# Two attention mixers with heads interleaved, one aligned slab pool and one more held chunk of output weights

## The chip, the cores and the metric

The kernel runs on one NeuronCore of one Trainium2 chip, as one program. The time is device time of that core, in microseconds, the median of several executions. The engines are TensorE (PE, matrix products), its weight loader (PEld in the profile), VectorE (DVE), ScalarE (ACT), GpSimd (POOL) and SyncE (SP), which issues most of the DMA transfers here. Each engine takes its own instructions strictly in the order in which they stand in its queue.

## The reference

The program computes two transformer blocks of two layers each on 512 tokens of width 1024, all in fp32. The second block has besides a context of 256 tokens. What the change touches lies in the second block, whose first layer mixes tokens with a window attention (8 heads, beside a Fourier mix), and whose second layer mixes them with a neighbourhood attention (16 heads). Cut to that:

```python
def _window_attention(q, k, v, k_ctx, v_ctx, sink):      # first layer ("even")
    ...
    s_win = jnp.einsum('bnqkgd,bnjkd->bnkgqj', qb, kw).astype(jnp.float32) * scale
    s_ctx = jnp.einsum('bnqkgd,bjkd->bnkgqj', qb, k_ctx).astype(jnp.float32) * scale
    ...
    p = jax.nn.softmax(jnp.concatenate([s_win, s_ctx, sk], axis=-1), axis=-1).astype(v.dtype)
    o = (jnp.einsum('bnkgqj,bnjkd->bnqkgd', p[..., :nw], vw)
         + jnp.einsum('bnkgqj,bjkd->bnqkgd', p[..., nw:nw + C], v_ctx))

def _neighbourhood_attention(q, k, v, k_ctx, v_ctx, rel_bias):   # second layer ("odd"), per row r of 64 tokens
    ...
        s_nb = jnp.einsum('bqhd,bjhd->bhqj', q_row, k_rows).astype(jnp.float32) * scale + bias[None]
        s_nb = jnp.where(mask[None, None], s_nb, NEG_2)
        s_cx = jnp.einsum('bqhd,bjhd->bhqj', q_row, k_ctx).astype(jnp.float32) * scale
        p = jax.nn.softmax(jnp.concatenate([s_nb, s_cx], axis=-1), axis=-1).astype(v.dtype)
        return (jnp.einsum('bhqj,bjhd->bqhd', p[..., :n], v_rows)
                + jnp.einsum('bhqj,bjhd->bqhd', p[..., n:], v_ctx))

    for i in range(DEPTH):                                # second_block
        ...
        x = x + g1 * o
        h = _rms(x, norm2_g[i]) * (1.0 + sc2) + sh2
        x = x + g2 * _swiglu(h, ffn_w_gate[i], ffn_w_up[i], ffn_w_down[i])
```

The context heads (`_ctx_attention`) attend from the 256 context tokens to themselves, in the first layer alone. `o` is the attention's output times an output matrix of 1024 x 1024 (`ev_w_out`, `od_w_out`).

## The kernel before

**Products.** An fp32 product is made of three products of rounded halves: every operand is split into a high half (a cast on ACT) and the rest (a subtraction on DVE), and `mm3` (L188 to L192) multiplies high by high (L190), high by low (L191) and low by high (L192). Weights come from HBM in pieces of 128 x 1024 into four raw buffers `wr`; `weight` (L145) issues the load on SP, casts to `wh` on ACT (L160) and subtracts to `wl` on DVE (L161), three buffers each. With `held=True` the halves go to slabs instead and stay. `split` (L169, its two instructions L172 and L173) does the same for activations: `xq` are split inputs of a projection, `mgh`, `hdh`, `yah`, `ybh`, `ycl` split intermediate results of the first block (h and l for the halves), `cath` and `catl` split outputs of attention, `pth` and `ptl` split transposed softmax weights.

**PSUM.** Eight banks of 128 x 512: four with tag A for attention, four with tag G for projections.

**Stages in time.** First block: mixer to 560 us, FFN to 950, mixer to 1510, FFN to 1925. Second block: the even layer's context heads until 2030 or so, its window attention 2070 to 2245, the rest of its mixer to 2375, its FFN to 2720, a transition to 2775; the odd mixer's attention in four groups of four heads that begin at 2771, 2854, 2937 and 3020, the end of its mixer 3110 to 3145, its FFN 3145 to 3500.

**Filling.** Attention leaves PE gaps while softmax runs on the other engines. So the projections for the next group are written as generators in a queue; `fill(us)` (L128) draws matmuls from it until so many microseconds, by the code's own rates, are used up. Where `fill` stands in the code decides what stands between two steps of attention on PE; the scheduler that builds the program then may move single instructions.

**An odd head** (`s1` L1472, `s2` L1514, the loop behind it). `s1` makes scores for four query tiles: two stacked products of 256 columns each (L433, L434) into one bank, neighbourhood keys in its left half and context keys in its right; DVE adds mask and bias and takes the maximum in one instruction; ACT makes the exponentials (one of 512 columns, L1498, for tiles 0 and 3; two of 256, L1504 and L1506, for tiles 1 and 2); then `fill(0.85)`. The bias of a head is loaded by three DMAs and prepared on GpSimd (L1481). The operands are *stacks*: every two heads, `stacks` transposes queries and keys (ten blocks) and splits them on ACT and DVE into 128-row tiles `stk` and `low` (L403 and after). `s2` calls `window_av` (L1012) for the head before: two context blocks and three window blocks, each of them transposes of exponentials into one bank (L1020 or L1029), split into `pth` and `ptl`, `fill(0.85)`, and the products with the values into one bank `po` that is held for the whole head (L1024 or L1038). `fold` then copies `po` into `ya` (L482), and after each second head `over_sums` divides by the sums. In the loop all four score blocks of a head come first and then the five blocks of the head before; groups do not overlap: the last head of a group has its `window_av` alone.

**The output matrix of the odd layer.** Its 1024 rows are four chunks `w[hf, 0..3]` for each half `hf` of the columns. Chunks 0 to 2 need the heads of groups 0 to 2 and are multiplied as filling in the last group (`out_part`); chunk 3 is loaded and split there, and multiplied in `out_end`, two half-chunks for each of four token tiles and two halves, after the last head. Behind each tile come its residual sum, its norm and its transposes (L298) for the FFN.

**The even layer's heads** (`heads` L1288 with `c1`, `c2` for the context and `s1`, `s2` for the window) run the same way, with fills of 2.0 and 3.0 us, and 1.3 us. In the window attention each of the four query tiles has two banks of scores, two maxima and two exponentials.

**Slabs.** `phase` opens one pool a stage; `F` gives slabs of 128 x 512 fp32, `R` the same for split halves, each tag with its own number of buffers (`MIX1`, `FFN1` and so on). Small tiles are in the same pool. In the program as built `wh`, `wl` and `xq` begin at 64 bytes past a multiple of 128 in each partition; the slabs of the first block begin at a multiple of 128, those of the even mixer and of the second block's FFNs at 64 past it.

Of the kernel before, what the change touches and what calls it, by code (L numbers as in the profile page):

```python
# [9 lines left out]
F32 = mybir.dt.float32  # L10
# [31 lines left out]
FFN1 = dict(F=18, R=34)  # L42
FFN1B = dict(F=17, R=28)
CF = (2.0, 3.0)
EVEN = dict(F=21, R=25, L=2)
FFN2 = dict(F=18, R=30)
ODD = dict(F=18, R=23, L=4)
# [6 lines left out]
class Gen:  # L54
    def __init__(self, ctx, tc, t):
# [14 lines left out]
        nc.vector.memset(self.ones, 1.0)  # L70

    def phase(self, ctx, name, **bufs):
        self.bufs, self.pending = bufs, {}
        self.ph = ctx.enter_context(self.tc.tile_pool(name=name, bufs=1))
        self.lows, self.turn = {}, {}

    def tile(self, tag, name, shape, dt=F32):
        return self.ph.tile(list(shape), dt, name=name, tag=tag, bufs=self.bufs[tag])

    def F(self, name, n=512):  # L80
        return self.tile("F", name, [128, 512])[:, :n]

    def R(self, name, n=512):
        return self.tile("R", name, [128, 512], F32R)[:, :n]
# [51 lines left out]
    def drain(self, gen=None):  # L136
# [4 lines left out]
        while self.fq:  # L141
            self.drain(self.fq.pop(0))

# [276 lines left out]
    def low(self, n):  # L420

        if n not in self.lows:
            self.lows[n] = [self.small(f"low{n}_{i}", [128, n], F32R, bufs=1) for i in range(self.bufs["L"])]
# [588 lines left out]
    def window_av(self, es, ident, fill, vst, vctx):  # L1012
# [3 lines left out]
        hl, where = [], {}  # L1016
        for cb in range(2):
# [4 lines left out]
            self.fill(fill)  # L1022
            for a in range(2):
                nc.tensor.matmul(po, vctx[cb], ph[a], start=(cb == 0 and a == 0), stop=False)  # L1024
        for b, blocks in enumerate(self.WP):
# [7 lines left out]
            self.fill(fill)  # L1033
            for kb in sorted({k for k, _ in blocks}):
                qs = [i for k, i in blocks if k == kb]
                o = blocks.index((kb, qs[0])) * 128
                for a, p in enumerate((h, l)):
                    nc.tensor.matmul(po[:, qs[0] * 128:qs[-1] * 128 + 128], vst[kb], p[:, o:o + len(qs) * 128],  # L1038
                                     start=False, stop=(b == 2 and a == 1))
        return po  # L1040
# [199 lines left out]
    def even(self, sc, sx, y):  # L1240
# [16 lines left out]
        def c1(h, qs, rc):  # L1257
# [8 lines left out]
            for i in range(2):  # L1266
                nc.scalar.activation(e[:, i * 256:i * 256 + 256], ps[:, i * 256:i * 256 + 256], AF.Exp,
                                     bias=nm[:, i:i + 1], accum_out=sm[:, i:i + 1])
            self.sink_sum(rc[:, :, h % 2], nm, [sm], sink, h, 2)
            self.fill(CF[0])  # L1270
            return e

        def c2(h, e, ya):
# [6 lines left out]
            self.fill(CF[1])  # L1280
# [7 lines left out]
        def heads(z, scale, new, s1, s2, cat):  # L1288
            qs, ya, rc, prev = {}, {}, {}, None
            for h in range(9):  # L1290
                if h < 8:
                    if h % 2 == 0:
# [3 lines left out]
                        ya[h // 2] = new(h // 2)  # L1296
                        rc[h // 2] = self.small(f"rcp{len(z)}", [128, len(z), 2])
                    es = s1(h, qs[h], rc[h // 2])
                if prev is not None:
                    j = (h - 1) // 2  # L1300
                    s2(h - 1, prev, ya[j])
                    if h % 2 == 0:
                        self.over_sums(ya[j], rc[j], self.ident)
                        if cat is not None:
                            cat[4 + j] = self.split_r(ya[j], "cat")
                prev = es
# [85 lines left out]
    def odd(self, sc, st):  # L1392
# [63 lines left out]
        for gr in range(4):  # L1456
# [5 lines left out]
            def stacks(hp):  # L1462
# [6 lines left out]
                for e in range(2):  # L1469
                    st_[hp * 2 + e] = q2[e], k2[e], c2[e]  # L1470
# [338 lines left out]
```

## Time and profile before

| what | value |
|---|---|
| time, median of 3 runs | 3507.51 us (3503.96, 3509.67, 3507.51) |
| profiled execution, its own time | 3504.4 us |
| its span (first to last instruction) | 3502.6 us |
| PE busy | 98% |
| PEld busy | 84% |
| DVE busy | 62% |
| ACT busy | 45% |
| POOL busy | 8% |

The busy shares are means over all stages. PE's records overlap (a matmul starts before the last one ends), and their ends are modelled, so its share hides short waits; those are read stage by stage from what the weight loader waited for. DMA moves 115 GB/s over the span, with 16 engines busy about a third of the time.

### The profile page before, as it was taken

To read this page: it belongs to the slowest core of one execution; us is meant where nothing else is said; L and a number is where in the kernel's file an instruction comes from. 1 tells how busy PE (TensorE), PEld (TensorE's weight loads), DVE (VectorE), ACT (ScalarE), POOL (GpSimd) and SP (SyncE) were. 2 spreads that over 40 slices of the span, in tenths; PEclk is the share of its full clock that TensorE was granted. 3 is DMA by queue.
4 is the path that set the end of the run, shared out by engine and by line. 5 is a ranking of instruction groups with operands and counts; after the bars stand their busy time and mean duration, and the time that the engine had idled before them with its cause. 6 is when DMAs were issued, how large, how long until landed. Compare 5 with 4: busy or idle time off the path is not lost.

```text
span 3502.6 us, 48430 instructions
## 1 busy us (share of the span) xinstructions
PE 3425.0 (98%) x18702; PEld 2937.6 (84%) x18702; DVE 2185.0 (62%) x3599; ACT 1561.5 (45%) x2933; POOL 278.6 (8%) x524
## 2 busy tenths in 40 slices
PE   8999999999999999999999999999999999989999
PEld 8888888888888888888887888988888888878887
DVE  5567645999564775579857777774334566673433
ACT  5445424424364554344334567653222466652222
POOL 2200000000021000000001200000000333300000
PEclk9999999999999999999999999999999999999999
DMA  4221124675323212446743233463323322333222
GB/s 124 83 91 55 67 96 152 199 228 181 106 81 92 79 60 73 132 146 216 256 136 121 73 109 121 145 205 109 102 96 115 96 55 55 67 107 119 96 90 87
DMA packets 144646, 404.49 MB, mean 115 GB/s; under 512 B 26752, under 2 KB 35104, under 8 KB 144416
## 3 DMA queue, kind: packets, MB, share of 16 engines
q1 hardware_dynamic: 144416, 401.40, 36.1%
q8 instruction: 147, 2.41, 0.3%
q14 instruction: 83, 0.68, 0.1%
HBM read 384.46 MB, written 16.88 MB: 115 GB/s over the span
## 4 chain that ended last, share of the span: by engine, by line
PE 85%; DVE 5%; ACT 4%; issue 3%; POOL 2%; DMA 1%; SPq 0%; POOLq 0%; ACTq 0%; DVEq 0%
PE ps L190 25%; PE ps L191 25%; PE ps L192 25%; PE ps L433 1%; PE ps L434 1%; PE ps L466 1%; PE ps L776 1%; ACT stk L403 1%; PE ps L1038 1%; DVE wl L161 1%; PE ps L298 1%; PE ps L1024 1%; PE ps L685 1%; PE ps L1029 1%; POOL hrms L331 1%
## 5 line engine op out<-in xcount | busy, mean ns | idle before, releaser
L160 ACT CAST wh<-wr 128x1024 fp32r<-128x1024 f32 (+2 forms) x540 | 557.3, 1032 | 1115.4 <-PE ps L191 499.9
L161 DVE TENSOR_TENSOR wl<-wr,wh 128x1024 fp32r<-128x1024 f32 (+2 forms) x540 | 651.4, 1207 | 581.5 <-ACT wh L160 573.5
L190 PE MATMUL ps<-xq,wh 128*128 128x512 f32 (+1 forms) x2664 | 956.7, 360 | 8.5 <-ACT xq L172 6.7
L191 PE MATMUL ps<-xq,wh 128*128 128x512 f32 (+1 forms) x2664 | 945.2, 355 | 0.9 <-DVE xq L173 0.8
L192 PE MATMUL ps<-xq,wl 128*128 128x512 f32 (+1 forms) x2664 | 945.5, 355 | 0.1
L190 PEld LDWEIGHTS ps<-xq,wh 128*128 128x128 f32 x2664 | 505.9, 190 | 73.7 <-ACT xq L172 8.6
L192 PEld LDWEIGHTS ps<-xq,wl 128*128 128x128 f32 x2664 | 505.5, 190 | 69.0 <-DVE wl L161 0.3
L191 PEld LDWEIGHTS ps<-xq,wh 128*128 128x128 f32 x2664 | 505.8, 190 | 64.9 <-DVE xq L173 1.8
L190 PE MATMUL ps<-wh,xq 128*128 128x256 f32 (+3 forms) x1056 | 342.5, 325 | 2.5 <-ACT wh L160 1.3
L191 PE MATMUL ps<-wl,xq 128*128 128x256 f32 (+3 forms) x1056 | 335.1, 318 | 1.6 <-DVE wl L161 0.9
L192 PE MATMUL ps<-wh,xq 128*128 128x256 f32 (+3 forms) x1056 | 335.4, 318 | 0.7 <-DVE xq L173 0.7
L191 PE MATMUL ps<-wl,hdh 128*128 128x512 f32 x704 | 275.4, 391 | 0.0
L190 PE MATMUL ps<-wh,hdh 128*128 128x512 f32 x704 | 275.1, 391 | 0.0
L192 PE MATMUL ps<-wh,hdl 128*128 128x512 f32 x704 | 273.9, 389 | 0.0
L190 PEld LDWEIGHTS ps<-wh,xq 128*128 128x128 f32 x1056 | 202.8, 192 | 10.2 <-ACT ngate L534 1.8
L191 PEld LDWEIGHTS ps<-wl,xq 128*128 128x128 f32 x1056 | 202.5, 192 | 8.3 <-DVE wl L161 1.1
L192 PEld LDWEIGHTS ps<-wh,xq 128*128 128x128 f32 x1056 | 202.1, 191 | 7.6 <-DVE xq L173 0.9
L906 DVE SCALAR_TENSOR_TENSOR adaj<-adaw,cb 128x1024 bf16<-128x1024 f32 x160 | 194.7, 1217 | 16.5 <-DMA adaw<-in_ada_w_dram 15.8
L173 DVE TENSOR_TENSOR ptl<-ps,pth 128x512 fp32r<-128x512 f32 (+1 forms) x208 | 132.9, 653 | 52.3 <-ACT pth L172 50.7
L172 ACT CAST pth<-ps 128x512 fp32r<-128x512 f32 (+1 forms) x208 | 114.9, 573 | 94.3 <-PE ps L466 45.9
L190 PEld LDWEIGHTS ps<-wh,hdh 128*128 128x128 f32 x704 | 132.2, 188 | 28.8
L192 PEld LDWEIGHTS ps<-wh,hdl 128*128 128x128 f32 x704 | 132.1, 188 | 28.1
(438 smaller groups left out, 5302.7 us busy)
## 6 DMA issues: line engine op xcount, KB each, us to landing
wr<-in_ffn_w_gu_dram SPq DMA_DIRECT2D x132, 512.0 KB, 3.3
wr<-in_ffn_w_down_dram SPq DMA_DIRECT2D x110, 512.0 KB, 3.3
adaw<-in_ada_w_dram SPq DMA_DIRECT2D x96, 512.0 KB, 4.2
wr<-in_ffn_w_up_dram SPq DMA_DIRECT2D x88, 512.0 KB, 3.9
wr<-in_w_in_g_dram SPq DMA_DIRECT2D x48, 512.0 KB, 3.3
xd<-x SPq DMA_DIRECT2D x56, 256.0 KB, 2.0
x<-xd SPq DMA_DIRECT2D x56, 256.0 KB, 5.8
wr<-in_w_in_d_dram SPq DMA_DIRECT2D x32, 384.0 KB, 3.2
```

The source lines that it names most:

```text
L160: nc.scalar.copy(h, r)
L161: nc.vector.tensor_sub(l, r, raw(h))
L172: nc.scalar.copy(hi, src)
L173: nc.vector.tensor_sub(lo, src, raw(hi))
L190: mm(out, lh, rh, start=start, stop=False)
L191: mm(out, lh, rl, start=False, stop=False)
L192: mm(out, ll, rh, start=False, stop=stop)
L298: nc.tensor.transpose(ps[:, q * 128:q * 128 + 128], xn[hf][:, q * 128:q * 128 + 128], self.ident)
L331: e.tensor_tensor(out, out, self.mhalf.to_broadcast(list(out.shape)), op=OP.pow)
L403: nc.scalar.activation(dst, ps[own], AF.Copy, scale=scale[own])
L433: mm(out, q, k[0][:, ks], start=True, stop=False)
L906: nc.vector.scalar_tensor_tensor(j, w, 1.0, cb[s], op0=OP.mult, op1=OP.mult, accum_out=acc[s][:, m:m + 1])
```

## The change

- **`weave` and generators.** `window_av`, `c1`, `c2` and both `s1` become generators with a step for each block. A new method `weave(gens, us)` takes one step of each in turn, with `fill(us)` after every step. For each head it gets the last head's `window_av` and the next head's `s1`: a block of the last head's transposes, filling, a block of the next head's scores, filling, and so on.
- **Value products a group later.** In a step `window_av` transposes and splits block b and then multiplies block b-1 with its values.
- **Fills.** 1.3 us a step in the window attention (as before), 2.5 for the context heads, 1.05 in odd groups 0 to 2 and 0.55 in the last.
- **Window scores.** Query tiles 0 and 3 (256 window keys) have window and context scores in one bank, one maximum and one exponential of 512 columns. The sums are cleared on GpSimd ahead.
- **Slab pool.** Slabs of both kinds get one tag S in a pool of their own, opened ahead of the pool of small tiles, with the same number of buffers in all; `low` tiles and the table `dftc` lie there too. A tile `pad` of 16 floats a partition in the constants moves what follows by 64 bytes. In the program as built, `wh`, `wl`, `xq` and all slabs begin at multiples of 256 bytes.
- **Output weights of the odd layer.** `out_part` multiplies chunks 0 and 1 alone; chunk 2 is loaded there with `held=True` into eight slabs in all, and `out_end` multiplies four half-chunks a tile and half in place of two.
- **Odd loop.** One loop over 17 steps in place of four times five, with the same bounds of groups.

```diff
+PAD = 16
-EF = (1.3, 1.3, 1.3)
-OF = (0.85, 0.85, 0.85)
-MIX1 = dict(F=26, R=28, L=4)
...
+EF = 1.3
+OF = (1.05, 0.55)
+MIX1 = dict(S=54, L=4)
...
     def phase(self, ctx, name, **bufs):
+        self.sp = ctx.enter_context(self.tc.tile_pool(name=name + "s", bufs=1))
         self.ph = ctx.enter_context(self.tc.tile_pool(name=name, bufs=1))
     def F(self, name, n=512):
-        return self.tile("F", name, [128, 512])[:, :n]
+        return self.tile("S", name, [128, 512])[:, :n]
...
+    def weave(self, gens, us):
+        gens = [g for g in gens if g is not None]
+        while gens:
+            for g in list(gens):
+                try:
+                    next(g)
+                except StopIteration:
+                    gens.remove(g)
+                else:
+                    self.fill(us)
...
-    def window_av(self, es, ident, fill, vst, vctx):
+    def window_av(self, es, ident, vst, vctx, done):
...
+        for make, b in ((ctx, 0), (ctx, 1), (window, 0), (window, 1), (window, 2)):
+            av = make(b)
+            if last is not None:
+                last()
+            last = av
+            yield
+        last()
+        done(po)
+        yield
...
-                pw, pc = self.P(), self.P()
+                one = n == 256
+                pw = self.P()
+                pc = pw[:, 256:512] if one else self.P()[:, :256]
...
-                yield from self.gated([(w[hf, c], 2) for c in range(3)], lambda k: cat[k], NT, x, hf, g, "G", 1, None)
-            ws.extend(self.weight(w[hf, 3], (128, 2, 512)) for hf in range(2))
+                yield from self.gated([(w[hf, c], 2) for c in range(2)], lambda k: cat[k], NT, x, hf, g, "G", 1, None)
+            for hf in range(2):
+                ws.append([self.weight(w[hf, 2], (128, 2, 512), True), self.weight(w[hf, 3], (128, 2, 512))])
...
-                    for kk in range(2):
-                        ts = slice(i * 128, i * 128 + 128)
-                        self.mm3(ps, cat[6 + kk][0][:, ts], cat[6 + kk][1][:, ts], ws[hf][0][:, kk], ws[hf][1][:, kk],
-                                 kk == 0, kk == 1)
+                    for k, (wh, wl) in enumerate(((h2[0], l2[0]), (h2[1], l2[1]), (h3[:, 0], l3[:, 0]),
+                                                  (h3[:, 1], l3[:, 1]))):
+                        self.mm3(ps, cat[4 + k][0][:, ts], cat[4 + k][1][:, ts], wh, wl, k == 0, k == 3)
...
+        for h in range(17):
+            gr, hl = divmod(h, 4)
+            if h and hl == 0:
+                self.weave([av(h - 1)], OF[gr == 4])
+                over(h // 2 - 1)
+            if h < 16:
...
+                self.weave([av(h - 1) if hl else None, s1(h, stk.pop(h), rc[h // 2], es[h])], OF[gr == 3])
```

ScalarE, the second head of odd group 1 (before): `ew` and `ec` are exponentials of window and context, `onm` the maxima, `osum` the sums, `pth` the cast of a transposed block of the head ahead.

```order
L1498 ACTIVATE ew_26747,osum_26738<-ps_26740,onm_26745 128x512
L1504 ACTIVATE ew_26762,osum_26738<-ps_26755,onm_26760 128x256
L1506 ACTIVATE ec_26763,osum_26738<-ps_26755,onm_26760 128x256
L1504 ACTIVATE ew_26784,osum_26738<-ps_26777,onm_26782 128x256
L1506 ACTIVATE ec_26763,osum_26738<-ps_26777,onm_26782 128x256
L1498 ACTIVATE ew_26802,osum_26738<-ps_26795,onm_26800 128x512
L172 CAST pth_26821<-ps_26816 128x512
L172 CAST pth_26838<-ps_26833 128x512
L172 CAST pth_26864<-ps_26859 128x512
L172 CAST pth_26885<-ps_26881 128x384
L172 CAST pth_26901<-ps_26897 128x384
```

The same place on ScalarE in the changed program, where the cast is L188 and the exponentials are L1532, L1538 and L1540:

```order
L188 CAST pth_26725<-ps_26720 128x512
L1532 ACTIVATE ew_26753,osum_26744<-ps_26746,onm_26751 128x512
L188 CAST pth_26772<-ps_26767 128x512
L1538 ACTIVATE ew_26794,osum_26744<-ps_26787,onm_26792 128x256
L1540 ACTIVATE ec_26795,osum_26744<-ps_26787,onm_26792 128x256
L188 CAST pth_26820<-ps_26815 128x512
L1538 ACTIVATE ew_26842,osum_26744<-ps_26835,onm_26840 128x256
L1540 ACTIVATE ec_26795,osum_26744<-ps_26835,onm_26840 128x256
L188 CAST pth_26860<-ps_26856 128x384
L1532 ACTIVATE ew_26884,osum_26744<-ps_26877,onm_26882 128x512
L188 CAST pth_26904<-ps_26900 128x384
```

The five casts of a head moved from behind all six exponentials of the next head to between them.

TensorE, in the last odd group (before): L1029 transposes a window block, L1024 and L1038 multiply by values `vs`, L190 to L192 are filling (`cath`, `catl` outputs of heads by weights `wh`, `wl`).

```order
L1029 MATMUL ps_28887<-rident_25052,ew_28774 128x128
L1024 MATMUL ps_28858<-pth_28878,vs_28648 128x512
L1029 MATMUL ps_28906<-rident_25052,ew_28714 128x128
L1029 MATMUL ps_28906<-rident_25052,ew_28743 128x128
L1029 MATMUL ps_28906<-rident_25052,ew_28759 128x128
L191 MATMUL ps_28721<-wl_28930,cath_28560 128x512
L192 MATMUL ps_28721<-wh_28929,catl_28561 128x512
L190 MATMUL ps_28722<-wh_28929,cath_28223 128x512
L191 MATMUL ps_28722<-wl_28930,cath_28223 128x512
L1024 MATMUL ps_28858<-ptl_28879,vs_28648 128x512
```

TensorE, in the last odd group of the changed program: L450 and L451 are scores, L1052 transposes of a window block, L1044 products with values.

```order
L1044 MATMUL ps_28759<-ptl_28766,vs_28626 128x512
L450 MATMUL ps_28803<-stk_28664,stk_28652 128x256
L451 MATMUL ps_28803<-low512_1_25555,stk_28652 128x256
L450 MATMUL ps_28803<-stk_28671,stk_28652 128x256
L451 MATMUL ps_28803<-low256_1_25574,stk_28652 128x256
L1052 MATMUL ps_28819<-rident_25033,ew_28695 128x128
L1052 MATMUL ps_28819<-rident_25033,ew_28721 128x128
L1052 MATMUL ps_28819<-rident_25033,ew_28737 128x128
L1052 MATMUL ps_28819<-rident_25033,ew_28752 128x128
L1044 MATMUL ps_28759<-pth_28794,vs_28629 128x512
L1044 MATMUL ps_28759<-ptl_28795,vs_28629 128x512
```

Before, four matmuls of filling stand ahead of a low product of the same block; in the changed program a block of scores and one of transposes stand between the products of two blocks, with no filling here.

## Rows read from the trace of the kernel before

**Rows 1.** The page's first part: busy us, share, instructions of each engine.

```profile
PE 3425.0 (98%) x18702; PEld 2937.6 (84%) x18702; DVE 2185.0 (62%) x3599; ACT 1561.5 (45%) x2933; POOL 278.6 (8%) x524
```

**Rows 2.** Windows: window attention, odd attention, end of odd mixer. Columns stand first.

```profile
core 0: us, PE busy (x) PEld busy (x) DVE busy (x) ACT busy (x) POOL busy (x), PEclk, DMA share, GB/s
2070.00:2245.00 175.00, 173.17 (x1232) 156.35 (x1232) 133.10 (x267) 134.48 (x277) 3.37 (x4) 1.00 0.37 121
2775.00:3110.00 335.00, 318.44 (x2305) 289.51 (x2303) 222.27 (x401) 205.09 (x460) 100.81 (x163) 1.00 0.29 69
3110.00:3145.00 35.00, 24.17 (x143) 21.49 (x143) 27.50 (x45) 19.08 (x44) 4.14 (x8) 0.85 0.31 106
```

**Rows 3.** PEld's waits, odd groups 0-2: for whom, us in total, times, longest.

```profile
PEld ps L1024 <- ACT pth L172: 7.5, 7, 1.7
PEld ps L1024 <- DVE ptl L173: 6.7, 12, 1.0
PEld ps L433 <- ACT stk L403: 4.9, 10, 0.6
PEld ps L433 <- issue: 2.7, 9, 0.3
```

**Rows 4.** PEld's waits, the last odd group, 3020 to 3110 us.

```profile
PEld ps L433 <- ACT stk L403: 2.2, 4, 0.7
PEld ps L1024 <- ACT pth L172: 2.0, 7, 0.4
```

**Rows 5.** Timeline near 2890: start, us, engine, instruction [idle before, releaser].

```profile
2888.99 2.21 POOL L1481 TENSOR_TENSOR nam<-namask,nab 128x744 f32<-128x744 f32 x1 [30.98 <-DVE onm L1494]
...
2889.42 2.87 DVE L161 TENSOR_TENSOR wl<-wr,wh 128x1024 fp32r<-128x1024 f32 x1
...
2891.69 0.27 PE L1020 MATMUL ps<-rident,ew 128*128 128x128 f32 x1
...
2892.98 0.47 ACT L1504 ACTIVATE ew<-ps,onm 128x256 f32<-128x256 f32 x1 [1.77 <-DVE osum L1510]
...
2895.46 0.60 ACT L172 CAST pth<-ps 128x512 fp32r<-128x512 f32 x1
...
2896.11 0.50 PE L1024 MATMUL ps<-pth,vs 128*128 128x512 f32 x1 [1.53 <-ACT pth L172]
```

**Rows 6.** Lines by form, odd group 1: busy, mean ns, idle before.

```profile
L173 DVE TENSOR_TENSOR ptl<-ps,pth 128x512 fp32r<-128x512 f32 x12 | 8.1, 680 | 3.3 <-ACT pth L172 3.3
L172 ACT CAST pth<-ps 128x512 fp32r<-128x512 f32 x12 | 7.1, 606 | 4.3 <-PE ps L1029 2.2 <-PE ps L1020 2.1
```

**Rows 7.** Matmul forms (whole run twice; 690-925; 3150-3500); two timeline rows.

```profile
L191 PE MATMUL ps<-wl,mgh 128*128 128x512 f32 x128 | 50.8, 397 | 0.0
...
L191 PE MATMUL ps<-ycl,wh 128*128 128x512 f32 x64 | 25.2, 394 | 0.0
...
L191 PE MATMUL ps<-wl,hdh 128*128 128x512 f32 x142 | 55.9, 394 | 0.0
...
L191 PE MATMUL ps<-wl,hdh 128*128 128x512 f32 x176 | 68.5, 389 | 0.0
...
698.68 0.39 PE L192 MATMUL ps<-wh,hdl 128*128 128x512 f32 x1
698.91 0.39 PE L190 MATMUL ps<-wh,hdh 128*128 128x512 f32 x1
```

**Rows 8.** PEld's waits, end of the odd mixer, 3110 to 3145 us.

```profile
PEld ps L298 <- issue: 7.8, 2, 7.5
PEld ps L190 <- ACT cath L172: 2.5, 1, 2.5
PEld ps L190 <- ACT xq L172: 1.8, 1, 1.8
```

**Rows 9.** PEld's waits for ACT, window attention, 2070 to 2245 us.

```profile
PEld ps L1024 <- ACT pth L172: 2.1, 7, 0.5
```

**Rows 10.** PEld's waits, context heads, 1945 to 2030 us.

```profile
PEld ps L1284 <- ACT pth L172: 4.5, 6, 3.0
```

More of the change, by code (lines that the diff above doesn't have):

```diff
@@ L422, in low @@
         if n not in self.lows:
-            self.lows[n] = [self.small(f"low{n}_{i}", [128, n], F32R, bufs=1) for i in range(self.bufs["L"])]
+            self.lows[n] = [self.sp.tile([128, n], F32R, name=f"low{n}_{i}", tag=f"low{n}_{i}", bufs=1)
+                            for i in range(self.bufs["L"])]
             self.turn[n] = 0
@@ L1010, with ctx @@
     WP = (((0, 0), (0, 1), (3, 2), (3, 3)), ((1, 0), (1, 1), (1, 2)), ((2, 1), (2, 2), (2, 3)))
-    def window_av(self, es, ident, fill, vst, vctx):
+    def window_av(self, es, ident, vst, vctx, done):
         nc = self.nc
         po = self.P()
-        hl, where = [], {}
-        for cb in range(2):
+        last = None
+        def ctx(cb):
             p = self.P()
@@ L1021, in window_av, with av, window @@
             ph = self.split_r(p, "pt")
[L1022 to L1025, printed above, removed]
+            def av():
+                for a in range(2):
+                    nc.tensor.matmul(po, vctx[cb], ph[a], start=(cb == 0 and a == 0), stop=False)
+            return av
+        def window(b):
+            blocks = self.WP[b]
             ps = self.P()
@@ L1286, in c2, with heads @@
             self.fold(ya, po, h % 2)
-        def heads(z, scale, new, s1, s2, cat):
-            qs, ya, rc, prev = {}, {}, {}, None
+        def heads(z, scale, new, s1, s2, cat, us):
+            qs, ya, rc, es = {}, {}, {}, {}
             for h in range(9):
+                j = h // 2
                 if h < 8:
@@ L1451, in odd, with stacks @@
         g, ws = [], []
+        def stacks(zq, zk, hp):
+            qt = self.heads_t(zq, hp * 128, self.rident)
+            q2 = [self.stack(qt, e, False, gcol[:, 0:1]) for e in range(2)]
+            kt_ = self.heads_t(zk[2:], hp * 128)
+            k2 = [self.stack(kt_, e, True, gcol[:, 1:2]) for e in range(2)]
+            kt_ = self.heads_t(zk[:2], hp * 128)
+            c2 = [self.stack(kt_, e, True, gcol[:, 1:2]) for e in range(2)]
+            return [(q2[e], k2[e], c2[e]) for e in range(2)]
@@ L1536, in odd @@
+        self.drain()
         self.drain(out_end())
@@ L1624, in emit @@
             g.wmask = g.const("wmask", BF, pool=g.ph)
-            w = g.const("dftc", pool=g.ph)
+            w = g.F("dftc", 256)
+            g.load(w, t["c_dftc"])
             g.dftc = [g.small(f"dftc{i}", [128, 256], F32R, bufs=1) for i in range(2)]
```

250 lines of the change are left out of this document (123 added, 127 removed).

## The prediction

> **What bounds the kernel now.** I read the page's first line first: TensorE (PE) is marked busy for 3425.0 of 3502.6 us [rows 1]. Matmuls overlap and their ends are modelled, so this hides short waits; what PE loses is better read from its weight loads (PEld), which are short and show a gap where a matmul starts late. Then the table by stage [rows 2]: in the last stretch of the odd mixer PE is marked busy for only 24.17 of 35 us, in the odd attention 318.44 of 335, in the window attention 173.17 of 175. The change works in these stages, on PE's own path. VectorE (DVE) and ScalarE (ACT) are busy for two thirds of the odd attention (222.27 and 205.09 of 335) and three quarters of the window attention (133.10 and 134.48 of 175), so neither is the bound there; they are what PE waits for.
>
> For whom it waits, the waits of PEld say. In odd groups 0 to 2 the value products (L1024) wait 7.5 us for ACT's high half and 6.7 us for DVE's low half of the transposed weights, the scores (L433) 4.9 us for the stacked keys and queries and 2.7 us without a named releaser [rows 3]. The last group has less of the first kind: 2.0 us, beside 2.2 for stacks [rows 4].
>
> One wait in full [rows 5]: the transposes of a head's context block end soon after 2891.69. Their cast on ACT starts only at 2895.46 and the value product at 2896.11, after 1.53 us of idle PE. In between ACT is not slow, it is in order: the exponentials of the next head's scores stand ahead of the cast, and they wait themselves, 1.77 us, behind DVE, whose subtraction of 2.87 us began while GpSimd's bias operation of 2.21 us ran. Alone the path is short: 0.606 us for the cast, 0.680 for the subtraction [rows 6], so about 1.3 us and two hand-overs.
>
> **The change, part by part.** I work from the profiled run (3504.4 us; span 3502.6) and move the result to the median of the runs shown, 3507.5.
>
> *Turns, and value products a group later (odd groups 0 to 2).* The order of ACT in the section on the change shows the effect: before, five casts pth stand in a row behind all six exponentials of the next head; now each stands between the exponentials of two score blocks. On PE a transposed block now has ahead of its value product one block of scores, the next block's transposes and two portions of filling of 1.05 us by the code, where it had one of 0.85. That is 2.1 us of filling alone against the 1.3 us of the path, while a cast waits behind one score block's exponentials. Of 14.2 us of value waits [rows 3], with 1.7 more in rows of L1038 that I leave out, I expect 3 to 5 us to stay, where GpSimd holds DVE. That gives **-11 us**; bounds: -14, all gone, and 0, if they only move. The scores after the ten stack transposes at a new pair of heads get less cover, since transposes of the last head and their casts now share the queue with the stacks. 7.6 us wait there now; they may lose 2 or gain 5 us, and I take **+1**.
>
> *Last odd group and the end of the mixer.* One of the three chunks of output weights that were multiplied as filling in the last group is now held in slabs and multiplied in out_end: 2 halves x 2 blocks x 4 token tiles x 3 = 48 matmuls of 512 columns. Two that follow each other start 0.23 us apart [rows 7], so 11 us of PE work move. Where they arrive, PE stands still: in 3110 to 3145 PEld waits 7.8 us at the transposes (L298), 2.5 us for the last cat and 1.8 us for xq [rows 8]. DVE works there for 27.50 of 35 us [rows 2]. An output tile now costs PE 2.8 us in place of 1.4, in step with DVE, so the rows of token tiles 0 and 1 are normalised while PE still multiplies 2 and 3. Of 12.1 us I expect 3 to stay: **-9** (bounds -11 and -3). Where they leave, filling falls to 0.55 us a turn, and the second order in that section shows a stretch of the last group without any: transposes, four score matmuls, products. There ACT and DVE set the pace. Some ten blocks that wait 0.4 us give **+4** (bounds -1 and +13, ten or so that wait as long as the one of rows 5). The moved weights' DMA stays at its place in SP's queue; the cast of a chunk becomes two halves on ACT and on DVE, at equal element counts.
>
> *One slab pool, aligned.* In the program as built, the weight tiles wh and wl and the operands xq begin 64 bytes past a multiple of 128; the slabs of the first block's mixers and FFNs begin at a multiple of 128, those of the even mixer and of both last FFNs at 64 past, as the weights do. In the changed program all begin at multiples of 256. Rows of one shape tell what that costs [rows 7]: a 512-column matmul takes 389 ns in the last FFN, where both operands lie alike, and 397 (mgh), 394 (ycl) and 394 (hdh, first block) where they lie 64 bytes apart. Timeline rows put starts of the latter some 6 ns further apart too, though a row of 0.01 us can't show it singly. 384 matmuls of mg at 7 ns, 576 of ya, yb and yc at 5, and 352 triples of the first FFNs, at 8 ns a triple, make 2.7 + 2.9 + 2.8 = 8.4 us. These stages run without gaps: **-8** (bounds 0 and -10).
>
> The Trainium skill speaks against this term: "TensorE: Matmul & The Clock Gate", section "Step-by-step: what each phase is for", gives PE two independent read ports in SBUF, so that loading the next weights takes nothing from the running matmul. By that where they lie should not matter and the term would be 0. The rows differ by 5 to 8 ns all the same, in stages that differ in more than addresses; the rule is the second rival below.
>
> *Window attention.* The same turns, and for two of four query tiles one reduction and one exponential of 512 columns in place of two each. DVE and ACT are not the bound [rows 2], so this saves only what waits behind them. Value products wait 2.1 us for ACT there [rows 9] and, in a row I leave out, 0.8 for DVE: **-1.5** (bounds +3, as at the odd stacks, and -3). *Context heads:* 4.5 us of waits, 3.0 of them once [rows 10], while DVE works through the rotation of zq; the order still puts a rotation ahead there, so **0** (-4 to +3). At nothing: the pad, the constants in slabs and eight memsets on GpSimd, which works 3.37 of 175 us there [rows 2]; without that cover each would cost under 0.2 us.
>
> Sum: -11 + 1 - 9 + 4 - 8 - 1.5 + 0 = -24.5, and 3507.5 - 24.5 = **3483 us**.
>
> **The rivals.** *Waits only move.* ACT and DVE stay in order and GpSimd still holds DVE once a head; the value products then wait as long, a group later. For it: 2.87 us in [rows 5]. Against it: the cast no longer stands behind a whole head's exponentials. Without the -11, +1 and -1.5 the time is 3507.5 - 8 - 9 + 4 = 3494.5. *Addresses don't matter* (the page's rule, as a mechanism: the 5 to 8 ns come from what else those stages read): 3491. *The last group starves:* its term is +13 and the end gives 4, not 9: 3483 + 9 + 5 = 3497. *More goes:* value, stack and context waits vanish (-15, -5, -4), windows -4, end -9, addresses -8, last group 0: 3462.5. *Slower:* PE has four PSUM banks for attention. One is held by the sum po for the whole head, and now a transposed block, the next one and a score block share three; before, scores and transposes came one after the other. If each of 64 odd and 32 window score blocks waits w for a bank, the loss is 96 w against 13 us from addresses, end and last group. It decides from w = 0.14 us; at 0.4 us it is 38 us and 3533. For it: each bank is held for a score block's reduction, exponential and their queues. Against it: no PE row of the trace waits for a bank in these stages, and with filling a turn lasts over 3 us.
>
> **How the numbers follow.** Forecast 3483: 0.46. Waits only move 0.14, addresses don't matter 0.08, last group starves 0.13, more goes 0.11, slower 0.08. The range 3466 to 3503 holds the forecast with the errors of its terms (some 10 us together) and the first three rivals; it leaves out 3462.5 and 3533, 0.19 together. A measurement of this kernel can tell 0.2% from no change, 7 us: faster is under 3500.5, slower over 3514.5. The forecast gives 0.44 to faster and 0.02 to same; of the rivals in turn 0.11, 0.07, 0.09 and 0.11 are faster, 0.03, 0.01, 0.04 and 0 are the same, and the slow one gives 0.01 to same and 0.07 to slower. Together 0.82, 0.11 and 0.07.
>
> **What would show it.** In the changed trace the rows of mgh, ycl and hdh should stand at 389 to 391 ns; if they stay at 394 to 397 the address term is wrong. The waits of the value products for ACT and DVE should fall from 14.2 to about 4 us in groups 0 to 2 and rise in the last; those for stacks should stay near 7. The stretch after the last head should have PE busy at over 0.9 of its time, the 7.8 us at L298 gone. Waits of the scores or transposes for an exponential of an earlier block would be the slow rival. The forecast fails if the waits come from something that stands between transposes and products whatever the order, GpSimd's hold on DVE above all.

## The result and the profile after

The changed kernel takes 3556.9 us against 3508.2, a ratio of 1.0137 (interval 1.0117 to 1.0157): slower by 48 us, where 24.5 us of gain were forecast and the range ended at 3503. One more run of it fell in a slow state, at 6811.29 us, and is in none of these numbers. The profiled execution of the changed kernel has a span of 3554.9 us. The page's first part, which answers to [rows 1], shows that this is no more work: PE, DVE and ACT are as busy as before, within 16 us, over a span that is 52 us longer.

```profile
PE 3440.8 (97%) x18702; PEld 2956.1 (83%) x18702; DVE 2184.1 (61%) x3585; ACT 1568.4 (44%) x2907; POOL 282.2 (8%) x533
```

Where the time went is read from landmarks, the start of a matmul that both traces have (us from the start; the e columns are experiments below):

| landmark on PE | before | after | e1 two tags | e2 before, one tag | e3 before, aligned |
|---|---|---|---|---|---|
| first product with `mgh` | 533.5 | 543.1 | 530.6 | 543.9 | 532.5 |
| first transpose of the context heads' keys | 1939.4 | 1953.4 | 1929.0 | 1956.2 | 1933.6 |
| first mask of the window attention | 2070.0 | 2084.4 | 2060.8 | 2094.8 | 2065.9 |
| first product with split outputs of heads | 2321.0 | 2344.5 | 2309.4 | 2356.2 | 2317.0 |
| first transpose of odd group 0 | 2792.6 | 2825.5 | 2781.0 | 2834.3 | 2786.6 |
| last normalising transpose of the odd layer | 3107.6 | 3162.8 | 3110.1 | 3168.2 | 3101.5 |
| last product | 3497.9 | 3550.2 | 3499.5 | 3559.0 | 3493.0 |

33 of the 52 us are lost before the odd attention begins, 10 of them in the first mixer, of whose code the change touches the slab pool alone. The odd attention loses 22 more and the end gains 3.

**The first mixer.** PEld's and PE's waits of the stretch to 190 us (whom, us, times, longest) have two rows with no like before:

```profile
PEld ps L450 <- issue: 6.6, 3, 2.4
PE ps L450 <- DVE stk L423: 5.6, 3, 2.0
```

VectorE's timeline near 65 us (start, us, line, instruction, idle before) shows why the stacked operands come late:

```profile
64.43 0.69 DVE L423 TENSOR_TENSOR stk<-ps,stk 64x512 fp32r<-64x512 f32 x1
67.41 1.07 DVE L676 TENSOR_TENSOR do<-do,drs 128x512 f32<-128x512 f32 x1 [2.30 <-DMA drs<-dr]
68.51 0.69 DVE L423 TENSOR_TENSOR stk<-ps,stk 64x512 fp32r<-64x512 f32 x1
69.24 0.68 DVE L423 TENSOR_TENSOR low<-ps,stk 64x512 fp32r<-64x512 f32 x1
```

The multiplication L676 waits 2.30 us for a DMA and holds the next stack's halves behind it. In the kernel before, the same multiplication (L659 there) stood behind both stacks and the first maxima, and waited for nothing:

```profile
67.10 0.69 DVE L407 TENSOR_TENSOR low<-ps,stk 64x512 fp32r<-64x512 f32 x1
...
68.82 1.07 DVE L659 TENSOR_TENSOR do<-do,drs 128x512 f32<-128x512 f32 x1
```

**The end of the second block's first FFN.** PE's and ACT's timeline, after:

```profile
2742.07 0.39 PE L208 MATMUL ps<-wh,hdl 128*128 128x512 f32 x1
2748.58 0.79 PE L206 MATMUL ps<-wh,hdh 128*128 128x512 f32 x1 [6.12 <-ACT wh L171]
2749.30 0.79 PE L207 MATMUL ps<-wl,hdh 128*128 128x512 f32 x1
...
2742.37 0.63 ACT L963 ACTIVATE junk<-x 128x512 f32<-128x512 f32 x1 [2.68 <-DVE x L1130]
...
2747.93 3.20 ACT L171 CAST wh<-wr 128x512 fp32r<-128x512 f32 x6
```

L171 casts held weights (slabs of split halves) for the last half of the down projection. They stand behind L963, which writes fp32 slabs from the first half's results, so PE has run out of weights for 6.12 us. In the program as built, the slab of the first of these casts had last been read at 2640.6 us by the same trace: memory was free 107 us earlier. The order alone is in the way.

The second row shows a cost beyond the stop: 0.79 us for a matmul that took 0.39 before it. The stretches from 2742 to 2749 us and on to 2753 (columns as in [rows 2]) have granted clocks of 0.77 and 0.55, part of them at the lower of the two levels (1.2 of 2.4 GHz):

```profile
2742.00:2749.00 7.00, 0.88 (x4) 0.32 (x2) 5.64 (x9) 4.71 (x12) 0.00 (x0) 0.77 0.68 226
2749.00:2753.00 4.00, 4.00 (x11) 2.93 (x10) 3.26 (x6) 2.13 (x5) 0.00 (x0) 0.55 0.79 269
```

Over the whole span the granted clock is 0.988 after and 0.996 before, a difference worth at most 0.008 x 3555 = 28 us at full speed, an estimate; part of it lies inside the stops, where PE does nothing, so it can't be added to their length.

**The odd mixer.** The stages of [rows 2] after (same columns), and the first of the three stops of PE in groups 0 to 2 beside what GpSimd does ahead of it:

```profile
2084.00:2260.00 176.00, 175.24 (x1258) 159.41 (x1258) 131.44 (x255) 138.38 (x251) 2.98 (x9) 1.00 0.37 123
2810.00:3163.00 353.00, 314.06 (x2238) 288.34 (x2237) 223.29 (x403) 205.12 (x459) 100.18 (x162) 0.97 0.28 63
3163.00:3198.00 35.00, 34.48 (x206) 29.82 (x206) 27.40 (x44) 18.97 (x43) 4.28 (x8) 1.00 0.32 113
```

```profile
2865.82 0.20 POOL L346 TENSOR_SCALAR hrms<-hrms 128x8 f32<-128x8 f32 x1 [13.14 <-DVE hrms L994]
...
2874.38 1.04 POOL L999 TENSOR_TENSOR z<-z,hrms 128x512 f32<-128x512 f32 x1
...
2875.55 2.93 POOL L1516 TENSOR_TENSOR nam<-namask,nab 128x744 f32<-128x744 f32 x1
...
2878.67 0.61 POOL L507 COPY rb<-orc 128x512 f32<-128x512 f32 x1
...
2879.34 1.12 PE L511 MATMUL ps<-rident,rb 128*128 128x128 f32 x4 [4.50 <-POOL rb L507]
```

The last stretch is as forecast: PE is busy for 34.48 of 35 us there, 24.17 before [rows 2], and the wait at the transposes [rows 8] is gone. But L507, which spreads the reciprocal sums for the normalising transposes, stands at the end of 13 us of GpSimd work without a gap: norms of three of the next group's projections and the next head's bias. In the kernel before, the first such copy of group 0 (L490 there) stood behind one such norm and ahead of two, and was done 1 us before PE came for it:

```profile
2837.71 0.61 POOL L490 COPY rb<-orc 128x512 f32<-128x512 f32 x1
...
2839.31 0.49 PE L494 MATMUL ps<-rident,rb 128*128 128x128 f32 x3
```

PEld's waits after, groups 0 to 2 (2825 to 3085 us), which answer to [rows 3]:

```profile
PEld ps L511 <- POOL rb L507: 14.6, 3, 4.9
PEld ps L1044 <- DVE ptl L189: 4.3, 6, 1.5
PEld ps L450 <- ACT stk L419: 4.0, 10, 0.6
PEld ps L1062 <- DVE ptl L189: 3.2, 3, 1.1
```

and in the last group (3085 to 3163 us), which answer to [rows 4]:

```profile
PEld ps L1062 <- DVE ptl L189: 4.6, 7, 1.5
PEld ps L450 <- ACT stk L419: 4.1, 3, 2.2
PEld ps L1044 <- DVE ptl L189: 3.4, 5, 1.1
PEld ps L1044 <- ACT pth L188: 2.9, 3, 1.5
```

By their first transposes the groups of the kernel before begin at 2793, 2874, 2957 and 3040 us, some 20 us behind the times that its stages were given with; over the same stretches as here (2792 to 3040, 3040 to 3108) all waits of its value products come to 16.7 us and 3.5. In groups 0 to 2 they did fall, to 7.9, and the row for ACT's cast is gone from the longest; in the last group they rose to 10.9.

### The profile page after: what moved, and what is told of

Its sections match the earlier page's. It is cut to its first block, busy times and chain, and to the rows that moved or that the text cites. A ratio compares the mean times of both kernels' runs of the same rounds, so it can differ in the third digit from the quotient of the medians.

```text
span 3554.9 us, 48348 instructions
## 1 busy us (share of the span) xinstructions
PE 3440.8 (97%) x18702; PEld 2956.1 (83%) x18702; DVE 2184.1 (61%) x3585; ACT 1568.4 (44%) x2907; POOL 282.2 (8%) x533
## 5 line engine op out<-in xcount | busy, mean ns | idle before, releaser
L189 DVE TENSOR_TENSOR ptl<-ps,pth 128x512 fp32r<-128x512 f32 (+1 forms) x208 | 133.9, 653 | 50.8 <-ACT pth L188 49.0
L207 PEld LDWEIGHTS ps<-wl,hdh 128*128 128x128 f32 x704 | 132.6, 188 | 28.9 <-DVE wl L172 1.5
```

Of the source, the lines that this page charges most:

```text
L189: nc.vector.tensor_sub(lo, src, raw(hi))
L207: mm(out, lh, rl, start=False, stop=False)
```

## The experiments

**e1 and e2: one tag or two.** The first two stops above have one thing in common: an instruction that fills a slab of split halves stands behind one that fills an fp32 slab. Theory A: within one tag, slabs are handed out in the order of the code, so the two kinds can't pass each other any more. Rival B: the pool's new place. e1 gives the changed kernel its two tags back:

```diff
-MIX1 = dict(S=54, L=4)
+MIX1 = dict(F=26, R=28, L=4)
...
-ODD = dict(S=41, L=4)
+ODD = dict(F=16, R=25, L=4)
...
     def F(self, name, n=512):
-        return self.tile("S", name, [128, 512])[:, :n]
+        return self.tile("F", name, [128, 512])[:, :n]
     def R(self, name, n=512):
-        return self.tile("S", name, [128, 512], F32R)[:, :n]
+        return self.tile("R", name, [128, 512], F32R)[:, :n]
```

> The changed kernel with one edit: the slab pool keeps its place and alignment, but slabs of fp32 and of split halves get two tags again (F and R, with the counts of before; 16 and 25 in place of 18 and 23 in the odd mixer, 41 in all). Theory A, one tag hands slabs out in program order, so that a half that could be made early now waits behind an fp32 tile whose result comes late: the time that stages outside the odd mixer lost, 34 us by weight-load starts (with 8 of it hidden by the alignment's gain), comes back, 3557 - 42 = 3515, at most 3525. In the trace the 6 us stop before the transition to the odd layer and the stops at the stacks of the first mixer are gone. Rival B, the loss comes from the pool's new place (other addresses, small tiles apart): the time stays within 8 us of 3557.

3508.2 us, ratio 1.0002 (0.9993 to 1.0012): 49 us come back, 7 more than expected, and 44.5 of the 50.7 us between the two traces' last products (the table above) lie ahead of the odd attention. VectorE near 65 us in e1, beside the rows of after:

```profile
62.50 0.69 DVE L423 TENSOR_TENSOR stk<-ps,stk 64x512 fp32r<-64x512 f32 x1 [0.65 <-ACT stk L417]
63.69 0.68 DVE L423 TENSOR_TENSOR low<-ps,stk 64x512 fp32r<-64x512 f32 x1 [0.50 <-ACT stk L417]
...
66.15 0.69 DVE L423 TENSOR_TENSOR low<-ps,stk 64x512 fp32r<-64x512 f32 x1
...
67.88 1.07 DVE L676 TENSOR_TENSOR do<-do,drs 128x512 f32<-128x512 f32 x1
```

The multiplication is behind the stacks again and waits for nothing; the stacks wait for ACT alone. The held weights at the end of the FFN are cast ahead of the results of the first half:

```profile
2691.41 3.22 ACT L171 CAST wh<-wr 128x512 fp32r<-128x512 f32 x6
2704.75 0.63 ACT L963 ACTIVATE junk<-x 128x512 f32<-128x512 f32 x1 [2.68 <-DVE x L1130]
```

e2 does the opposite, the kernel before with one tag (the same lines the other way, in the old pool).

> The kernel before with one edit: its slabs get the one tag S with the changed kernel's counts, in the old pool; no interleaving, no pad, old output weights. Theory A: slower by about the 42 us that stages outside the odd mixer lost, 3540 to 3555. Rival B: no change, 3500 to 3512.

3566.6 us, ratio 1.0167 (1.0152 to 1.0183): 58 us slower with this one edit, more than the whole change and more than expected. 16.4 of the 58 are lost at the copy of the sums, as in the changed kernel (see e5); the rest is near the expected 42. Its PE waits have the same two stops, in the first mixer and at the end of the FFN:

```profile
PE ps L433 <- DVE stk L407: 5.9, 3, 2.1
...
PEld ps L190 <- ACT wh L155: 5.3, 1, 5.3
```

B falls, and of A the two runs show that the one tag costs 49 us in the new kernel and 58 in the old one; that it does so by the order rests on the rows that moved and moved back, and on e10.

**e10: number or order of slabs.** The changed kernel, with more slabs under its one tag:

```diff
-FFN1 = dict(S=52)
-FFN1B = dict(S=45)
+FFN1 = dict(S=56)
+FFN1B = dict(S=48)
...
-FFN2 = dict(S=48)
+FFN2 = dict(S=50)
```

> The changed kernel with more slabs under the one tag where memory allows it: 56 in place of 52 and 48 in place of 45 in the first block's FFNs, 50 in place of 48 in the second block's; the rest as changed. Theory A in its narrow form (the order in which slabs are handed out costs, not their number): 3550 to 3560. If too few slabs are the cause: the FFNs' part of the loss, some 8 to 15 us, comes back, 3542 to 3549.

3555.8 us, ratio 1.014 (1.0124 to 1.0155). In the three FFNs more memory gives back nothing that can be told (3556.9 without it). In the mixers there was no room to try it.

**e3: alignment alone.** The kernel before with the pad, and with the slab pool ahead of the small tiles, two tags kept:

```diff
+        self.pad = self.cp.tile([128, PAD], F32, name="pad", tag="pad")
+        nc.gpsimd.memset(self.pad, 0.0)
...
+        self.sp = ctx.enter_context(self.tc.tile_pool(name=name + "s", bufs=1))
...
-        return self.ph.tile(list(shape), dt, name=name, tag=tag, bufs=self.bufs[tag])
+        return self.sp.tile(list(shape), dt, name=name, tag=tag, bufs=self.bufs[tag])
```

> The kernel before with one edit: the pad and the slab pool ahead of the small tiles, with two tags as before, so that all slabs and weight tiles begin at multiples of 256 bytes; nothing else. If alignment is worth what the 512-column rows say (389 in place of 394 to 397 ns): 3507.5 - 8 = 3499.5 (3497 to 3502). Theory B (the new place of the pool costs 42 us): about 3540.

3498.6 us, ratio 0.9976 (0.9966 to 0.9986), so 8.4 us. Rows of one form in e3 (whole run twice, then 690 to 925), which answer to [rows 7]:

```profile
L195 PE MATMUL ps<-wl,mgh 128*128 128x512 f32 x128 | 50.2, 393 | 0.0
L195 PE MATMUL ps<-ycl,wh 128*128 128x512 f32 x64 | 24.9, 389 | 0.0
...
L195 PE MATMUL ps<-wl,hdh 128*128 128x512 f32 x145 | 56.4, 389 | 0.0
```

397, 394 and 394 ns became 393, 389 and 389, while the order of instructions differs from that of before in few rows (23 of 3599 on DVE, 9 of 2933 on ACT). In the changed kernel all three forms stand at 389. As the ends of matmuls are modelled, their starts are the better measure: matmuls of 512 columns that follow each other without a wait start 231 ns apart before and 227 in e3 and in the changed kernel for `mgh`, 233 and 227 for `ycl`, and 227.3 to 227.6 in all three for `xq` by `wh`, which lay alike before too.

**e4: the copy of the sums.** The changed kernel, one word changed in `over_sums`:

```diff
-        self.nc.gpsimd.tensor_copy(rb.rearrange("p (a d) -> p a d", d=64),
+        self.nc.vector.tensor_copy(rb.rearrange("p (a d) -> p a d", d=64),
```

> The changed kernel with one edit: the copy of the reciprocal sums ahead of the normalising transposes runs on VectorE in place of GpSimd. Theory C, PE stops once a group (14.6 us in three times) because this copy stands in GpSimd's queue behind a burst of norms and the bias of the next head: the stops go, and the half clock that follows them, 3557 - 15 - 4 = 3538 (3533 to 3545). Rival, something else is as late there: 3550 to 3560.

3537.2 us, ratio 1.0082 (1.0067 to 1.0097): 20 us less. The row of L511 is gone from the waits. Groups 0 to 2 are 18.0 us shorter (241.6 in place of 259.6), 3.4 more than that row held, and their granted clock is back at 1.00, from 0.97 (columns as in [rows 2], after and e4):

```profile
2825.00:3085.00 260.00, 236.84 (x1794) 225.22 (x1793) 160.43 (x287) 154.57 (x345) 87.77 (x137) 0.97 0.29 57
2826.00:3068.00 242.00, 231.11 (x1794) 219.46 (x1793) 163.30 (x292) 154.53 (x345) 85.16 (x131) 1.00 0.31 61
```

The same matmuls keep PE marked busy for 5.7 us less.

**e5: both mends.** e1 and e4 together.

> The changed kernel with both mends: two tags of slabs, and the copy of the reciprocal sums on VectorE. If the two causes are apart, the gains add: 3508 - 20 = 3488 (3484 to 3493). If the stop at the sums was a consequence of the one tag: 3500 to 3508.

3493.8 us, ratio 0.9962 (0.9947 to 0.9977). The gains add, less 6 us, so that the copy was late without the one tag too: PE lost 16.4 us at these transposes in e2 (old order, one tag), 15.2 in e1 (turns, two tags), 0.7 before. Each of the two edits alone is enough to put the copy late; by what path is not shown.

For the odd mixer the next runs need a finer measure. The table has, for three segments, the length (us) and in brackets what PE lost in it: the distance of each matmul's start to the next one's, less the distance that this form has where nothing waits. Segments run from landmark to landmark: the first transposes of groups 0 and 3, the last normalising transposes, the first down product of the FFN. Each line is one trace; kernels with the same code in groups 0 to 2 (e5, e6, e9) differ by up to 1.4 us there.

| kernel | groups 0 to 2 | last group | end |
|---|---|---|---|
| before | 247.9 (29.2) | 67.1 (7.3) | 116.6 (14.4) |
| after | 259.6 (41.0) | 77.7 (27.0) | 112.8 (1.6) |
| e5 both mends | 244.2 (25.6) | 74.0 (22.8) | 112.3 (1.5) |
| e6 e5, old output weights | 243.0 (24.3) | 73.9 (11.8) | 114.5 (14.7) |
| e7 e3, new output weights | 247.7 (29.0) | 64.0 (16.0) | 116.4 (2.4) |
| e8 e5, no turns | 243.1 (24.5) | 77.2 (25.9) | 112.3 (1.5) |
| e9 e5, last group in old order | 242.9 (24.2) | 77.5 (26.3) | 112.3 (1.5) |
| e11 e5, products not later | 245.1 (26.4) | 73.9 (22.7) | 112.3 (1.6) |
| e12 turns in the even layer only | 249.3 (30.6) | 64.0 (16.0) | 116.4 (2.5) |

**e6 and e7: the output weights.** e6 takes them back from e5, e7 adds them to e3 (old order of heads):

```diff
-                yield from self.gated([(w[hf, c], 2) for c in range(3)], lambda k: cat[k], NT, x, hf, g, "G", 1, None)
-            ws.extend(self.weight(w[hf, 3], (128, 2, 512)) for hf in range(2))
+                yield from self.gated([(w[hf, c], 2) for c in range(2)], lambda k: cat[k], NT, x, hf, g, "G", 1, None)
+            for hf in range(2):
+                ws.append([self.weight(w[hf, 2], (128, 2, 512), True), self.weight(w[hf, 3], (128, 2, 512))])
```

> As the run with both mends, but the output weights of the odd layer as before: three chunks multiplied as filling in the last group (0.85 us a step there), one held for the end. Theory D, the last group starves because its filling went to the end: its loss falls by 17 us, the end loses 10.6 us again, 3488 - 17 + 10.6 = 3482. Rival E, the last group starves by the turns whatever the filling: 3488 + 10 = 3498.

> The kernel before with the aligned pool of two tags (16 and 25 in the odd mixer) and with the changed kernel's output weights, in the old order of heads, with 0.57 us of filling at each place in the last group. Theory D: 3498.6 - 10.6 + 17 = 3505, since filling is missing there just the same. Rival E, the old order does without that filling: 3498.6 - 10.6 = 3488.

e6: 3494.4 us, 0.9961 (0.9946 to 0.9976), the same as e5. e7: 3495.0 us, 0.9962 (0.9949 to 0.9975), 4 us under e3, which these runs can't tell from no change (the intervals overlap). Neither D nor E forecast either time: both runs fell between the two. The table says why so little: the weights save 12 to 13 us at the end (14.4 to 2.4, 14.7 to 1.5) and cost 8.7 (e3 loses 7.3 in the last group as before does, e7 16.0) to 11.0 (e6 to e5) in the last group. Starving for lack of filling is what e7 shows, where heads take no turns: 16.0 us lost in place of 7.3. PEld's waits in its last group (3036 to 3101 us):

```profile
PEld ps L1029 <- ACT pth L176: 4.5, 6, 2.0
PEld ps L438 <- ACT stk L407: 2.8, 4, 1.4
PEld ps L1029 <- DVE ptl L177: 2.7, 4, 0.9
```

With the old weights the last group loses 11.8 us in e6 and 7.3 in the kernel before. The turns are not alone in these 4.5 us: e6 differs in the engine of the sums' copy and in the later products as well, and e9 below gains nothing by taking the turns back.

**e8 and e11: turns, and later products.** e8 runs `weave`'s generators one after the other, the scores first; e11 keeps turns and multiplies each block one filling after its own transposes:

```diff
 e8
-        while gens:
-            for g in list(gens):
...
+        for g in gens[::-1]:
+            for _ in g:
+                self.fill(us)
...
 e11
             av = make(b)
-            if last is not None:
-                last()
-            last = av
             yield
-        last()
+            av()
         done(po)
```

> As the run with both mends, but without turns: all four score blocks of a head, then the last head's blocks with value products a step later, in all three mixers. If the turns save waits (value products lost 14 us in groups 0 to 2 before and 7 after): 3488 + 7 = 3495 or more. If it is the later products alone: 3485 to 3491. If the turns themselves starve the last group: under 3480.

> As the run with both mends, with turns, but each block's value products in the step after its own transposes and filling, ahead of the next block's transposes. Without turns the time was 3504.6, with both 3493.8. If the turns alone bring what was gained: 3491 to 3497. If the products must also stand behind the next block's transposes (0.3 us more of cover against a path of 1.3 us): 3498 to 3505.

e8: 3504.6 us, 0.9993 (0.9983 to 1.0002). e11: 3495.5 us, 0.9960 (0.9946 to 0.9973), the same as e5. So with the products later, the turns are worth some 11 us; with turns, the later products are worth nothing that can be told. But the table shows no gain of turns in groups 0 to 2 (25.6 with, 24.5 without) and 3 us in the last group. They work in the even layer: from the first mask to the first product with split outputs e8 takes 255.1 us, e5 248.9 and e11 247.6, where the old order took 251.0 (before) to 251.2 (e7). For the context heads before it e8 takes 133.9 and e5 129.9, but there e7, in the old order, takes 130.0 and e3 132.3.

What turns and later products are worth together, e5 and e7 say: they have the same output weights and alignment, and differ in turns, later products, window scores and the engine of the sums' copy. Both have a ratio of 0.9962. Over the three segments e5 takes 430.5 us, e7 428.1 and the kernel before 431.6.

**e9 and e12: the old order where turns don't pay.** e9 is e5 with the last odd group in the old order; e12 has turns in the even layer alone, the odd layer as in e7, with the copy of the sums on GpSimd.

```diff
 e9
+        if not turns:
+            for g in gens[::-1]:
+                for _ in g:
+                    self.fill(us)
+            return
...
+                self.weave([av(h - 1) if hl else None, s1(h, stk.pop(h), rc[h // 2], es[h])], OF[gr == 3], gr < 3)
 e12
-OF = (1.05, 0.55)
+OF = (0.85, 0.57)
...
+                self.weave([av(h - 1) if hl else None, s1(h, stk.pop(h), rc[h // 2], es[h])], OF[gr == 3], False)
```

> As the run with both mends, but the last odd group in the old order (all scores of a head, then the last head's blocks, each with its filling and its own products), turns elsewhere, the new output weights kept. If the turns starve the last group (its attention and end took 186 us with turns and 180 in the old order with the same weights): 3493.8 - 6 = 3488. If what it lost lies elsewhere: 3492 to 3497.

> Two tags, aligned, new output weights; turns and later products in the even layer alone; the odd layer in the old order, with its old fillings (0.85, and 0.57 in the last group) and the copy of the sums on GpSimd. The old order with these weights took 3495.0 and lost 16 us in the last group; the even layer's turns gave 2 to 4 us beside it. If the parts add: 3492 (3490 to 3494). If the even layer's gain was not from the turns: 3495 to 3497.

e9: 3496.3 us, 0.9972 (0.9962 to 0.9982), the second of its two forecasts; its last group loses 26.3 us, more than with turns, so the turns inside it aren't what starves it. What separates it from e7's last group, 16.0 us with the same order in the code, is the group ahead of it, the engine of the sums' copy and fills of 0.55 in place of 0.57 us; which of them decides wasn't tried and stays open. e12: 3492.1 us, 0.9952 (0.9939 to 0.9965), at the forecast of the parts added up, and in the trace the even layer's segment takes 248.5 us against e7's 251.2. It is faster than the kernel before and the changed one, the fastest kernel here by its median, but its interval overlaps those of e5, e6, e7 and e11, so that by time the parts aren't shown to add.

## Why the prediction was wrong, point by point

**The step that failed: one pool, costed at nothing.** The prediction read the slab pool as a matter of addresses alone and gave the rest of it ("the pad, the constants in slabs") no price; that two tags became one isn't in the sum at all. It is worth +49 us (e1), twice the whole forecast gain, and lies mostly in stages that the working didn't look at. The orders that were shown ahead of the prediction are those of ACT and PE in the odd mixer; the rows that moved stand in DVE's order in the first mixer and in ACT's at the end of the FFN.

**The second miss: the copy of the sums.** The prediction looked for waits that ACT's and DVE's order made, and has GpSimd only as what holds DVE and as cover for eight memsets; the copy of the sums isn't in its sum. GpSimd is busy for no more than 100.81 of 335 us [rows 2], but at the place where it counts it works for 13 us without a gap, and PE waits at the end of it: +20 us in the changed kernel (e4), 14 with two tags (e1 to e5).

**Alignment, -8:** right, in its size and its rows. e3 changes addresses and little else and gains 8.4 us. By the rule of the Trainium skill that was weighed there ("TensorE: Matmul & The Clock Gate", section "Step-by-step: what each phase is for"), two independent read ports, it would be 0. The measurement decides against that for operands 64 bytes apart; what slows them no run here shows.

**Turns and later products, -11 + 1:** the mechanism was right for the value products, and the gain isn't there. They lost 14.8 us in groups 0 to 2 before, 7.6 after and 7.5 in e5; the prediction expected 3 to 5 to stay. With the mends the segment's whole loss falls by 3.6 us only, 29.2 to 25.6, since waits came up elsewhere, and the kernel with turns and later products is no faster than e7 without them. e5's waits in groups 0 to 2 (2787 to 3031 us):

```profile
PEld ps L450 <- ACT ew L1532: 4.5, 4, 1.8
PEld ps L450 <- ACT stk L419: 4.1, 10, 0.6
PEld ps L1062 <- DVE ptl L189: 3.8, 4, 1.1
PEld ps L1044 <- DVE ptl L189: 2.7, 2, 1.3
PEld ps L206 <- ACT sq L992: 2.4, 3, 0.9
```

The first row is the mechanism of the slow rival, scores that wait for an exponential of an earlier block: it exists, at 4 places of 48, and costs 4.5 us and not 38. The last is new too: filling waits for ACT to read filling's earlier results. It isn't made by the turns, for e8 has none and the same 2.4 us, while e11, with turns and the products not later, and e1, with the copy of the sums on GpSimd, have no such row; what makes it stays open. The stacks' 4.1 us are near the 4.9 of before [rows 3].

**Last group, +4, and end, -9:** the end gave more, 12 to 13 us; the last group took 15.5 in all (7.3 to 22.8 in e5), 8.7 to 11.0 of them for the weights. The rival that "starves" had the mechanism and nearly the price of the last group (+13), though not that of the end. The term failed because it priced ten waits like those of the rows of before, where filling stood; without it, transposes, scores and products all wait (e7's rows above).

**Window attention, -1.5, and context heads, 0:** e5 gains 2.2 us against e3 from the first mask to the first product with split outputs, near the forecast. For the context heads the traces show no difference beyond their scatter. That later products without turns would cost 4 us there against the old order (e8), wasn't foreseen.

Put together, the terms that were forecast as -24.5 came to about -14 with both mends (e5), 8.4 of them from alignment, and the two that weren't forecast to +63. In the odd mixer, where -15 was forecast, e5 is 1.1 us shorter than the kernel before. That e5's 3493.8 us lie at the 3494.5 of the rival "waits only move" is luck: the value products' waits did fall by half, and the end and the last group came out otherwise than that sum has them.

## What to carry to other kernels

Read a change of buffer tags as a change of order: where a scheduler hands out buffers of one tag in the order of the code, merging two tags ties kinds of work together that passed each other before, on every engine and in every stage that uses the pool. Look at the program's order in the stages that a change seems not to touch, and at each engine that PE waits for, however low its mean share. Filling that is moved to a gap leaves a gap behind: here 12 to 13 us were saved at the end and 9 to 11 us lost in the group before it.

## What the runs showed of the hardware

A stop of PE can cost more than its own length: behind the 6.12 us stop at 2742, matmuls of 512 columns took 0.79 us and then 0.63 in place of 0.39, at a granted clock of 0.55 from 2749 to 2753 us. Taking away three stops of 14.6 us together made groups 0 to 2 18.0 us shorter and put their granted clock from 0.97 to 1.00 (e4). And matmuls of 512 columns whose two operands begin 64 bytes apart, modulo 128, are marked with 394 to 397 ns in place of 389, and those of `mgh` and `ycl` start 4 and 6 ns further apart than 227; setting them alike gave 8.4 us over this kernel's stages (e3).
